# Channel-tile splits for the recurrence's input, long-convolution results kept in DRAM, and a new order of the seven Strassen products in a hybrid decoder layer

## The chip, the core and the metric

The kernel runs on one core of one Trainium2 chip. A core has five engines that take their instructions in parallel, each in its own order: TensorE (PE) for matrix products, VectorE (DVE), ScalarE (ACT), GpSimd (POOL), and SyncE (SP), which here only issues DMAs. The metric is the device time of one execution in microseconds (us), from a median of several runs. Work is in float32; each operand of a product is split into a high part (rounded to the type that TensorE takes) and a low remainder, and three products (high by high, high by low, low by high) stand for one.

## The reference, cut to what matters

One layer with 1024 positions and 1024 channels. The projection `z` has six parts, and two branches are computed from them:

```
h = rms_norm(x, g_mix)
z = h @ w_in + b_in
va, ga, xb, gb, sa, sb = split(z)          # 1024, 1024, 1536, 1536, 1024, 1024

u = causal_depthwise_conv(va * sigmoid(ga), conv_a_w)      # width 31
y_a = silu(layer_norm(u)) @ w_a_out

v = causal_depthwise_conv(xb, conv_b_w)                    # width 4
r, i = sigmoid(block_diag(v, w_a)), sigmoid(block_diag(v, w_x))   # 16 heads of 96 channels
v = linear_scan(a(r), mult(r) * i * v)                     # RG-LRU over the positions
y_b = (v * gelu(gb)) @ w_b_out

m = sigmoid(sa) * y_a + sigmoid(sb) * y_b
x = x + m @ w_o
x = x + square(relu(rms_norm(x) @ w_1)) @ w_2
out = rms_norm(x)
```

## The kernel before, in words

Channels lie on the 128 partitions and positions along a tile, so most tiles are 128x1024 (512 KB). They come from one pool, `acts`, with 35 buffers, which are given out in the order in which the program asks for them. A scheduler puts the instructions of each engine into one order ahead of time; `high_priority` and `high_priority(-LOWP)` move a block forward or back in it. At run time each engine and each issuing queue works through its order and waits where an input isn't there.

**First stage** (L367 to L561). `zchunk` (L377) makes 128 channels of `z` with 48 matmuls (8 slices of the contraction, three products, two halves) in one of three PSUM banks of tag `ps`. `xb_chunk` (L392) evacuates a chunk on ACT (L396) and applies the convolution of width 4: one pass on ACT (L399), three on VectorE (L404), result `v`, 12 tiles. `va_pair` (L493) makes a va and a ga chunk and joins them to `u` (L500 on ACT, L501 on VectorE). `conv` (L505) is the convolution of width 31: one pass on ACT (L513) and 30 passes, "taps", on VectorE (L516), each of which adds to the one before. The taps have low priority: they fill VectorE's gaps. Convolutions 0 to 4 start in this stage, 5 to 7 in the next. Each result, `y0` to `y7`, stays in a buffer of `acts` until the layer norm.

`rnn_steps` (L477) runs beside the chunks, a step after each. A head has 96 channels, which lie on one or two of the channel tiles (`PIECES`, L387). `rnn_load` (L415) moves the pieces of `v` into a 96x1024 tile of the pool `heads` (6 buffers) by DMAs on SP, and loads the head's weights. `rnn_split` (L427), one step later, splits the weights, and splits the head's input with `split_dma` (L64): ACT writes the negated high part, a DMA on POOL's queue adds the source to it, which leaves the low part, and ACT writes the high part again. `rnn_gates` (L436) has 12 matmuls (L444 to L446), two sigmoids (L448), and DMAs that bring the gates back to channel tiles (L453). `rnn_scan` (L455) does the recurrence for three channel tiles (four heads) at a time and stores the result in DRAM (`hd`).

**Strassen stage** (L566 to L694). The chunks of gb, sa and sb go in 14 pairs; each pair is one level of Strassen's scheme, in Winograd's form: seven products instead of eight, each 12 matmuls of 128x512 (`z_mm`, L624). The right-hand operands are the blocks of `h` and four sums of blocks, made by `x_sums` (L533) for each of two halves `c2`. The left-hand operands are made by `z_lhs` (L591): sums on VectorE (L598) and a split (L610 to L614). `z_step` (L652) issues a product, and after products 1 and 6 copies the bank on ACT into the bank on which later products accumulate (L656, L658). So product 6 needs the copy behind 1, and 5 and 3 the copy behind 6. `z_out` (L636) adds the bias, applies gelu or sigmoid, and stores to DRAM. The order of the products is written out by hand (`zseq`, L676 to L680); loads and left-hand operands are asked for up to four products ahead (L683). The pool `w` of this stage has 9 buffers, `evac` 5.

**yb and ya** (L696 to L798). `hg` is loaded from DRAM and split (12 tiles), and eight yb products run over it (L765 to L783). Between them stand three steps of the layer norm (`layer_norm_steps`, L727), behind yb 0, 3 and 5: the sum of the eight `y` on VectorE, the mean by a matmul with a constant matrix (`mu`) and the subtraction, the variance and the scaling. The last yb (L775) runs its three products slice by slice; the others use `mm3` (L85), which takes the low weights last. `split(ya[k], ...)` (L787) prepares the ya products (L788 to L795).

**Behind it** follow the output projection, the two products of the MLP (again Strassen's scheme) and the final norm.

Of the kernel before, what the change touches and what calls it, by code (L numbers as in the profile page):

```python
# [9 lines left out]
F32 = mybir.dt.float32  # L10
F32R = mybir.dt.float32r
# [19 lines left out]
def trunk_kernel(ctx: ExitStack, tc: tile.TileContext, x, xt_in, vecs, w_in, w_a_out, w_b_out,  # L31
# [13 lines left out]
    def T(name, dt=F32, shape=(P, S)):  # L45
        return tp.tile(list(shape), dt, tag="T", name=name)
# [4 lines left out]
    def split(src, h, l):  # L51
        nc.scalar.activation(h, src, AF.Copy)  # L52
        nc.vector.tensor_tensor(l, src, h.bitcast(F32), ALU.subtract)
# [10 lines left out]
    def split_dma(src, h, l):  # L64

        nc.scalar.activation(l, src, AF.Copy, scale=-1.0)  # L66
        nc.gpsimd.dma_start(l, src, accum_op=ALU.add)  # L67
        nc.scalar.activation(h, src, AF.Copy)
# [60 lines left out]
    def H(name, dt=F32):  # L129
        return qp.tile([HD, S], dt, tag="h", name=name)  # L130
# [278 lines left out]

    gws = {}  # L410
    parts = {}
    gate = {}
    hd = dp.tile([12, P, S], F32, name="hd")

    def rnn_load(n):  # L415
        g, hh = divmod(n, 4)
        v = H(f"v{n}")
        for (ti, p0, p1, d0) in PIECES[hh]:
            nc.sync.dma_start(v[d0:d0 + p1 - p0, :], vt[3 * g + ti][p0:p1, :])
        parts[n] = v  # L420
        raw = rp.tile([HD, 2, HD], F32, tag="rraw", name=f"rraw{n}")
        if n < 2:
            nc.gpsimd.tensor_copy(raw[0:1, 0, 0:1], vt[0][0:1, 0:1])
        nc.sync.dma_start(raw, w_rg[n])
        gws[n] = raw

    def rnn_split(n):  # L427
        gh = rp.tile([HD, 2, HD], F32R, tag="rh", name=f"rgh{n}")
        gl = rp.tile([HD, 2, HD], F32R, tag="rl", name=f"rgl{n}")
        split(gws[n], gh, gl)  # L430
        gws[n] = (gh, gl)
        vh, vl = H(f"vh{n}", F32R), H(f"vl{n}", F32R)
        split_dma(parts[n], vh, vl)
        parts[n] = vh, vl

    def rnn_gates(n):  # L436
        g, hh = divmod(n, 4)
# [39 lines left out]
    def rnn_steps():  # L477
        for n in range(-2, NH):
            if n >= 0:
                rnn_gates(n)  # L480
            if 0 <= n + 1 < NH:
                rnn_split(n + 1)
            if n + 2 < NH:
                while 3 * ((n + 2) // 4) + 2 not in vt:
                    yield
                rnn_load(n + 2)
            if n >= 0 and n % 4 == 3:
                rnn_scan(n // 4)
            yield

    ut, ya = {}, [None] * 8

    def va_pair(j):  # L493
        psv = zchunk(VA + j)
# [10 lines left out]
    def conv(j):  # L505
        u = ut.pop(j)
        acc = T(f"y{j}")

        def tap(d):
            w = WA - 1 - d  # L510
            return caw[:, w * 8 + j:w * 8 + j + 1]

        nc.scalar.activation(acc, u, AF.Identity, scale=tap(0), bias=cab_c[:, j:j + 1])  # L513
        with tc.high_priority(-LOWP):
            for d in range(1, WA):
                nc.vector.scalar_tensor_tensor(acc[:, d:S], u[:, 0:S - d], tap(d), acc[:, d:S],  # L516
                                               ALU.mult, ALU.add)
        ya[j] = acc

    rnn_it = rnn_steps()  # L520

# [8 lines left out]
    for p in (7, 6, 5, 4):  # L530
        xbh[p], xbl[p] = [None, None], [None, None]

    def x_sums(c2, last=()):  # L533
        q = {}
        for n, (hf, kk) in {12: (1, 0), 11: (0, 0), 22: (1, 1), 21: (0, 1)}.items():
            q[n] = wp.tile([P, S], F32, tag="w", name=f"xs{n}_{c2}") if n in last else \
                T(f"xs{n}_{c2}")
            nc.sync.dma_start(q[n], xu[hf, 2 * kk + c2])
        sub = nc.vector.tensor_tensor
        sub(q[11], q[12], q[11], ALU.subtract)  # L540
        sub(q[12], q[22], q[12], ALU.subtract)
        sub(q[22], q[22], q[11], ALU.subtract)
        sub(q[21], q[21], q[22], ALU.subtract)
        for p, n in ((7, 12), (6, 22), (5, 11), (4, 21)):
            xbh[p][c2] = h = T(f"xs{p}h_{c2}", F32R)
            nc.scalar.activation(h, q[n], AF.Copy)
            xbl[p][c2] = l = T(f"xs{p}l_{c2}", F32R)
            sub(l, q[n], h.bitcast(F32), ALU.subtract)

    for j in range(8):  # L550
        if j < 4:
            for i in range(3):
                xb_chunk(3 * j + i)
                step()
        va_pair(j)
        if j in CONVS:
            conv(CONVS[j])
        if j == 6:
            x_sums(0)
    for _ in rnn_it:  # L560
        pass  # L561

# [89 lines left out]
    def z_step(i, p):  # L652
        z_mm(i, p)
        with tc.high_priority():
# [17 lines left out]
                nc.vector.tensor_tensor(c, c, zb[i, "f"], ALU.add)  # L672
                z_out(i, 1, 0, c, "c")

    x_sums(1, (22, 21))
    zseq = [(0, 1), (1, 1), (0, 2), (1, 2), (0, 7), (0, 6), (0, 5), (1, 7), (0, 3), (0, 4),  # L676
            (1, 6), (1, 5)]
    for i in range(2, NZ):
        zseq += [(i, 1), (i - 1, 3), (i - 1, 4), (i, 7), (i, 6), (i, 2), (i, 5)]
    zseq += [(NZ - 1, 3), (NZ - 1, 4)]  # L680
    ready = 0
    for n, (i, p) in enumerate(zseq):
        while ready < min(len(zseq), n + 4):  # L683
            if zseq[ready][1] == 1:
                z_load(zseq[ready][0])
            z_lhs(*zseq[ready])
            ready += 1
        z_step(i, p)
        if p == 4 and i in (0, 2, 5):
            conv({0: 5, 2: 6, 5: 7}[i])  # L690
# [34 lines left out]
            hg.append((h, l))  # L725

    def layer_norm_steps():  # L727
        ssum = E("ssum")
        for j in range(1, 8):
            nc.vector.tensor_tensor(ssum, ya[0] if j == 1 else ssum, ya[j], ALU.add)  # L730
        yield
        pm = PS("mu", "ps2")
        for hs in HALVES:
            nc.tensor.matmul(pm[:, hs], onesm, ssum[:, hs], start=True, stop=True)
        vs, sq = E("vs"), E("sq")
        for j in range(8):
# [15 lines left out]
        yield  # L752

    ln_it = layer_norm_steps()
    wo = []

# [8 lines left out]
    for j in range(8):  # L765
        ws = wb0 if j == 0 else get_w(w_b_out[j, 0], f"wb{j}a") + get_w(w_b_out[j, 1], f"wb{j}b")
        sb = E(f"sb{j}")
        nc.gpsimd.dma_start(sb, spill[1, j])
        ps = PS(f"yb{j}")
        ops = [w + (wide(hg[k][0]), wide(hg[k][1])) for k, w in enumerate(ws)]  # L770
        if j < 7:
            mm3(ps, ops)
        else:

            for k, (wh, wl, ah, al) in enumerate(ops):  # L775
                for n, (a, b) in enumerate(((wh, ah), (wh, al), (wl, ah))):
                    for hf in range(2):
                        nc.tensor.matmul(ps[:, HALVES[hf]], a, b[hf], start=k == 0 and n == 0,
                                         stop=k == 11 and n == 2)
# [668 lines left out]
```

## Time and profile before

| what | value |
|---|---|
| median of 3 runs | 1702.7 us (1698.23 to 1703.65) |
| the profiled execution | 1702.45 us |
| its span, first to last instruction | 1700.6 us |
| mean granted clock of TensorE | 0.976 |
| ScalarE busy in the span | 891.1 us (52%) |
| GpSimd busy in the span | 214.5 us (13%) |
| first stage | to about 427 us |
| Strassen stage | about 427 to 735 us |
| yb, then ya | to about 885 and 985 us |

The span and the time of its own execution differ by 1.85 us, which lies before the first and after the last instruction. The page's rows for groups of instructions give the line, the engine, the operation, the written and the read names, the shapes, the count, the busy time and the mean duration in ns, and behind a bar the idle time of the engine just before them and what ended most of it. A row of the waits names who waited, for whom, the us in total, how often, and the longest. Where a helper records the instruction, the line is that of the helper: L92 is every `mm3`, L52 and L53 every `split`.

### The profile page before, as it was taken

How to read it: one execution, taken by the hardware profiler on the slowest of the kernel's cores; microseconds unless marked ns; L12 is line 12 of the kernel's file. 1: busy time of each engine (PE TensorE's matmuls, PEld its weight loads, DVE VectorE, ACT ScalarE, POOL GpSimd, SP SyncE). 2: the span in 40 equal slices, each digit the busy share in tenths (PEclk: the TensorE clock that was granted, in tenths of full speed). 3: DMA queues.
4: the chain of work that ended last, by engine and by line, in shares of the span. 5: the costliest groups of instructions: out<-in, count | busy, mean ns of one | idle time of the engine just before them, and what ended most of it. 6: DMA issues, size and time to landing. Idle time of an engine off the chain costs nothing. (4 is left out here: it accounts for less than half of the span.)

```text
span 1700.6 us, 18626 instructions
## 1 busy us (share of the span) xinstructions
PE 1601.7 (94%) x6910; PEld 1298.6 (76%) x6910; DVE 1146.5 (67%) x1329; ACT 891.1 (52%) x1157; POOL 214.5 (13%) x284
## 2 busy tenths in 40 slices
PE   8989889898799899989989999999999999999998
PEld 6867667677677677767868888778888888888886
DVE  6786788889988886354263315685555466888888
ACT  5548586773555555543354224564444457555553
POOL 0111010110223333311111000000000001111110
PEclk9989999999899999989999999999999999999999
DMA  9677776767587766773476255253332488888862
GB/s 364 147 159 176 170 177 141 188 142 224 130 217 204 184 162 168 175 248 100 101 214 175 74 149 173 79 182 124 112 112 99 138 261 205 216 231 213 217 142 99
DMA packets 94698, 288.63 MB, mean 170 GB/s; under 512 B 10976, under 2 KB 12512, under 8 KB 94608
## 3 DMA queue, kind: packets, MB, share of 16 engines
q1 hardware_dynamic: 59184, 180.77, 32.0%
q0 software_dynamic: 35280, 106.42, 29.6%
q8 instruction: 54, 0.88, 0.2%
q14 instruction: 36, 0.29, 0.1%
q10 hardware_dynamic: 144, 0.26, 0.0%
HBM read 139.82 MB, written 50.33 MB: 112 GB/s over the span
## 5 line engine op out<-in xcount | busy, mean ns | idle before, releaser
L516 DVE SCALAR_TENSOR_TENSOR y<-u,vec,y 128x1023 f32<-128x1023 f32 (+14 forms) x240 | 303.8, 1266 | 14.3 <-ACT y L513 10.2
L92 PE MATMUL z<-xh,win_h 128*128 128x512 f32 x400 | 131.0, 408 | 0.0
L92 PE MATMUL z<-xl,win_h 128*128 128x512 f32 x400 | 129.2, 403 | 0.0
L1244 DVE TENSOR_TENSOR acc<-acc,d 128x1024 f32<-128x1024 f32 x72 | 87.8, 1220 | 33.4 <-PE d L1232 32.8
L92 PE MATMUL z<-xh,win_l 128*128 128x512 f32 x400 | 94.8, 389 | 0.0
L92 PEld LDWEIGHTS z<-xh,win_h 128*128 128x128 f32 x400 | 79.6, 199 | 18.5 <-issue 0.2
L92 PEld LDWEIGHTS z<-xl,win_h 128*128 128x128 f32 x400 | 79.0, 197 | 18.1
L92 PEld LDWEIGHTS z<-xh,win_l 128*128 128x128 f32 x400 | 75.1, 188 | 15.6
L448 ACT ACTIVATE g<-rg,vec 96x1024 f32<-96x1024 f32 x32 | 35.6, 1112 | 65.1 <-PE rg L446 61.4
L446 PE MATMUL rg<-vl,rgh 96*96 96x512 f32 x64 | 29.2, 456 | 31.9 <-DMA vl<-v 31.9
L965 ACT ACTIVATE o<-s 128x512 fp32r<-128x512 f32 x64 | 38.1, 621 | 32.8 <-DVE s L957 28.2
L965 ACT ACTIVATE o<-w_raw 128x512 fp32r<-128x512 f32 x40 | 24.9, 624 | 51.7 <-DVE o L879 51.0
L781 DVE TENSOR_TENSOR m<-yb,sb 128x1024 f32<-128x1024 f32 x8 | 9.8, 1222 | 60.1 <-PE yb L92 47.7
L67 POOL DMA_DIRECT2D zo<-zw x42 | 37.1, 884 | 88.8 <-ACT zo L66 86.1
L67 POOL DMA_DIRECT2D db_1l<-wr x7 | 6.1, 867 | 327.2 <-ACT db_1l L66 304.7
L404 DVE SCALAR_TENSOR_TENSOR v<-xb,vec,v 128x1023 f32<-128x1023 f32 (+2 forms) x36 | 45.6, 1277 | 2.6 <-ACT v L399 2.6
L879 DVE TENSOR_TENSOR o<-s,o 128x512 fp32r<-128x512 f32 x64 | 42.4, 685 | 5.9 <-ACT o L965 5.8
L794 DVE TENSOR_TENSOR sa<-ya,sa 128x1024 f32<-128x1024 f32 x8 | 9.8, 1224 | 51.6 <-PE ya L92 51.6
L67 POOL DMA_DIRECT2D win_l<-win_raw x25 | 22.1, 883 | 176.8 <-ACT win_l L66 141.0
L863 DVE TENSOR_TENSOR x<-xr,o 128x1024 f32<-128x1024 f32 x8 | 9.7, 1219 | 51.4 <-PE o L831 37.2
L92 PE MATMUL ya<-suh,wa_h 128*128 128x512 f32 x128 | 40.0, 398 | 3.4 <-ACT suh L52 3.4
L446 PEld LDWEIGHTS rg<-vl,rgh 96*96 96x96 f32 x64 | 11.4, 178 | 41.5 <-DMA vl<-v 37.4
(1578 smaller groups left out, 4632.9 us busy)
## 6 DMA issues: line engine op xcount, KB each, us to landing
fr<-fd SPq DMA_DIRECT2D x32, 512.0 KB, 5.6
wr<-in_w_dram SPq DMA_DIRECT2D x32, 512.0 KB, 5.7
w_raw<-in_w_dram SPq DMA_DIRECT2D x31, 512.0 KB, 3.7
zw<-in_w_in_dram SPq DMA_DIRECT2D x28, 512.0 KB, 5.1
win_raw<-in_w_in_dram SPq DMA_DIRECT2D x25, 512.0 KB, 4.7
win_l<-win_raw POOLq DMA_DIRECT2D x25, 512.0 KB, 4.9
zo<-zw POOLq DMA_DIRECT2D x42, 256.0 KB, 3.6
fd<-fa SPq DMA_DIRECT2D x16, 512.0 KB, 3.3
```

The lines of the kernel that those rows point to most:

```text
L67: nc.gpsimd.dma_start(l, src, accum_op=ALU.add)
L92: nc.tensor.matmul(ps[:, HALVES[hf]], a, b[hf], start=i == 0, stop=i == len(todo) - 1)
L404: nc.vector.scalar_tensor_tensor(v[:, d:S], a[:, 0:S - d], cbw_c[:, w * 12 + t:w * 12 + t + 1], v[:, d:S], ALU.mult, ALU.add)
L446: nc.tensor.matmul(o, gh[:, gi, :], vl[:, hs], start=False, stop=True)
L448: nc.scalar.activation(a, ps[:HD, :], AF.Sigmoid, bias=(ba_c, bx_c)[gi][:, n:n + 1])
L516: nc.vector.scalar_tensor_tensor(acc[:, d:S], u[:, 0:S - d], tap(d), acc[:, d:S], ALU.mult, ALU.add)
L781: nc.vector.tensor_tensor(m[j], ps, sb, ALU.mult)
L794: nc.vector.tensor_tensor(sa, ps, sa, ALU.mult)
L863: nc.vector.tensor_tensor(x1, xr, ps, ALU.add)
L879: tt(l, src, h.bitcast(F32), ALU.subtract)
L965: nc.scalar.activation(o[:, 0], src, AF.Copy)
L1244: tt(acc[p, q2], acc[p, q2], ps, ALU.add)
```

## The change

It has four parts.

1. `rnn_load` splits each of the 12 tiles of `v` on the channel tiles (ACT copy, VectorE subtraction) and moves both parts to the heads' tiles by DMAs on SP. `rnn_split` is gone; the split of the heads' weights is in `rnn_load`, a step earlier.
2. `conv` stores each `y` in DRAM (`yd`) and adds it to `ysum` (for conv 0, an ACT copy starts it). The layer norm takes `ysum` for the mean and loads the `y` again as `yn`. It has two steps, behind yb 1 and 4.
3. `x_sums(0)` comes one pair earlier, `x_sums(1)` at the end of the first stage. In the Strassen stage the order of the seven products changes, loads are asked for seven products ahead, and the pools have 8 and 7 buffers for 9 and 5.
4. The last yb uses `mm3` too; three of the split tiles of ya take buffers of the pool `late`; one PSUM tag behind ya changes.

```diff
     def rnn_load(n):
         g, hh = divmod(n, 4)
-        v = H(f"v{n}")
+        parts[n] = H(f"vh{n}", F32R), H(f"vl{n}", F32R)
         for (ti, p0, p1, d0) in PIECES[hh]:
-            nc.sync.dma_start(v[d0:d0 + p1 - p0, :], vt[3 * g + ti][p0:p1, :])
-        parts[n] = v
+            t = 3 * g + ti
+            if t not in vp_:
+                vp_[t] = T(f"vth{t}", F32R), T(f"vtl{t}", F32R)
+                split(vt[t], *vp_[t])
+            for a, b in zip(parts[n], vp_[t]):
+                nc.sync.dma_start(a[d0:d0 + p1 - p0, :].bitcast(F32), b[p0:p1, :].bitcast(F32))
         raw = rp.tile([HD, 2, HD], F32, tag="rraw", name=f"rraw{n}")
...
-        gws[n] = raw
-
-    def rnn_split(n):
         gh = rp.tile([HD, 2, HD], F32R, tag="rh", name=f"rgh{n}")
         gl = rp.tile([HD, 2, HD], F32R, tag="rl", name=f"rgl{n}")
-        split(gws[n], gh, gl)
+        split(raw, gh, gl)
         gws[n] = (gh, gl)
-        vh, vl = H(f"vh{n}", F32R), H(f"vl{n}", F32R)
-        split_dma(parts[n], vh, vl)
-        parts[n] = vh, vl
...
         for n in range(-2, NH):
             if n >= 0:
                 rnn_gates(n)
-            if 0 <= n + 1 < NH:
-                rnn_split(n + 1)
             if n + 2 < NH:
...
             for d in range(1, WA):
                 nc.vector.scalar_tensor_tensor(acc[:, d:S], u[:, 0:S - d], tap(d), acc[:, d:S],
                                                ALU.mult, ALU.add)
-        ya[j] = acc
+            nc.sync.dma_start(yd[j], acc)
+            if j == 0:
+                ysum.append(T("ysum"))
+                nc.scalar.activation(ysum[0], acc, AF.Copy)
+            else:
+                nc.vector.tensor_tensor(ysum[0], ysum[0], acc, ALU.add)
...
-        for p, n in ((7, 12), (6, 22), (5, 11), (4, 21)):
+        for p, n in ((6, 22), (7, 12), (5, 11), (4, 21)):
...
-        if j == 6:
+        if j == 5:
             x_sums(0)
     for _ in rnn_it:
         pass
+    x_sums(1)
...
-    wp = stage.enter_context(tc.tile_pool(name="weights2", bufs=9, reuse_waits="tile"))
+    wp = stage.enter_context(tc.tile_pool(name="weights2", bufs=8, reuse_waits="tile"))
...
-    vp = stage.enter_context(tc.tile_pool(name="evac", bufs=5, reuse_waits="tile"))
+    vp = stage.enter_context(tc.tile_pool(name="evac", bufs=7, reuse_waits="tile"))
...
-    x_sums(1, (22, 21))
-    zseq = [(0, 1), (1, 1), (0, 2), (1, 2), (0, 7), (0, 6), (0, 5), (1, 7), (0, 3), (0, 4),
-            (1, 6), (1, 5)]
+    zseq = [(0, 1), (1, 1), (0, 2), (1, 2), (0, 6), (0, 7), (1, 7), (0, 5), (1, 6), (0, 3), (0, 4),
+            (1, 5)]
     for i in range(2, NZ):
-        zseq += [(i, 1), (i - 1, 3), (i - 1, 4), (i, 7), (i, 6), (i, 2), (i, 5)]
+        zseq += [(i, 1), (i, 7), (i - 1, 3), (i, 6), (i, 2), (i - 1, 4), (i, 5)]
     zseq += [(NZ - 1, 3), (NZ - 1, 4)]
-    ready = 0
+    loaded = ready = 0
     for n, (i, p) in enumerate(zseq):
+        while loaded < min(len(zseq), n + 7):
+            if zseq[loaded][1] == 1:
+                z_load(zseq[loaded][0])
+            loaded += 1
         while ready < min(len(zseq), n + 4):
-            if zseq[ready][1] == 1:
-                z_load(zseq[ready][0])
             z_lhs(*zseq[ready])
...
     def layer_norm_steps():
-        ssum = E("ssum")
-        for j in range(1, 8):
-            nc.vector.tensor_tensor(ssum, ya[0] if j == 1 else ssum, ya[j], ALU.add)
-        yield
         pm = PS("mu", "ps2")
         for hs in HALVES:
-            nc.tensor.matmul(pm[:, hs], onesm, ssum[:, hs], start=True, stop=True)
+            nc.tensor.matmul(pm[:, hs], onesm, ysum[0][:, hs], start=True, stop=True)
         vs, sq = E("vs"), E("sq")
         for j in range(8):
+            ya.append(T(f"yn{j}"))
+            nc.sync.dma_start(ya[j], yd[j])
...
-        ops = [w + (wide(hg[k][0]), wide(hg[k][1])) for k, w in enumerate(ws)]
-        if j < 7:
-            mm3(ps, ops)
-        else:
-
-            for k, (wh, wl, ah, al) in enumerate(ops):
-                for n, (a, b) in enumerate(((wh, ah), (wh, al), (wl, ah))):
...
+        mm3(ps, [w + (wide(hg[k][0]), wide(hg[k][1])) for k, w in enumerate(ws)])
...
-        if j in (0, 3, 5):
-            next(ln_it)
+        if j in (1, 4):
+            next(ln_it, None)
     su = []
     for k in range(8):
-        su.append((T(f"suh{k}", F32R), T(f"sul{k}", F32R)))
+        su.append(((E if k < 2 else T)(f"suh{k}", F32R), (E if k < 1 else T)(f"sul{k}", F32R)))
...
-            ps = PS(f"tr_m0{kk}{c2}", "ps2" if kk else "ps")
+            ps = PS(f"tr_m0{kk}{c2}", "ps2" if kk and c2 else "ps")
```

More of the change, by code (lines that the diff above doesn't have):

```diff
@@ L411, in trunk_kernel @@
     parts = {}
+    vp_ = {}
     gate = {}
@@ L489, in rnn_steps @@
             yield
-    ut, ya = {}, [None] * 8
+    ut = {}
+    yd = dp.tile([8, P, S], F32, name="yd")
+    ysum = []
     def va_pair(j):
@@ L531, in trunk_kernel, with x_sums @@
         xbh[p], xbl[p] = [None, None], [None, None]
-    def x_sums(c2, last=()):
+    def x_sums(c2):
         q = {}
         for n, (hf, kk) in {12: (1, 0), 11: (0, 0), 22: (1, 1), 21: (0, 1)}.items():
-            q[n] = wp.tile([P, S], F32, tag="w", name=f"xs{n}_{c2}") if n in last else \
-                T(f"xs{n}_{c2}")
+            q[n] = T(f"xs{n}_{c2}")
             nc.sync.dma_start(q[n], xu[hf, 2 * kk + c2])
@@ L751, in layer_norm_steps @@
                                  bias=lnb_c[:, j:j + 1])
-        yield
+    ya = []
     ln_it = layer_norm_steps()
@@ L769, in trunk_kernel @@
         ps = PS(f"yb{j}")
-        ops = [w + (wide(hg[k][0]), wide(hg[k][1])) for k, w in enumerate(ws)]
-        if j < 7:
-            mm3(ps, ops)
-        else:
-            for k, (wh, wl, ah, al) in enumerate(ops):
-                for n, (a, b) in enumerate(((wh, ah), (wh, al), (wl, ah))):
-                    for hf in range(2):
-                        nc.tensor.matmul(ps[:, HALVES[hf]], a, b[hf], start=k == 0 and n == 0,
-                                         stop=k == 11 and n == 2)
+        mm3(ps, [w + (wide(hg[k][0]), wide(hg[k][1])) for k, w in enumerate(ws)])
         m.append(T(f"m{j}"))
         nc.vector.tensor_tensor(m[j], ps, sb, ALU.mult)
-        if j in (0, 3, 5):
-            next(ln_it)
+        if j in (1, 4):
+            next(ln_it, None)
     su = []
     for k in range(8):
-        su.append((T(f"suh{k}", F32R), T(f"sul{k}", F32R)))
+        su.append(((E if k < 2 else T)(f"suh{k}", F32R), (E if k < 1 else T)(f"sul{k}", F32R)))
         split(ya[k], *su[k])
```

## The prediction

> **What bounds the kernel now.** I read the page first: the busy shares, the 40 slices and the costliest groups.
>
> ```profile
> span 1700.6 us, 18626 instructions
> PE 1601.7 (94%) x6910; PEld 1298.6 (76%) x6910; DVE 1146.5 (67%) x1329; ACT 891.1 (52%) x1157; POOL 214.5 (13%) x284
> ...
> PE   8989889898799899989989999999999999999998
> ...
> DVE  6786788889988886354263315685555466888888
> ...
> L516 DVE SCALAR_TENSOR_TENSOR y<-u,vec,y 128x1023 f32<-128x1023 f32 (+14 forms) x240 | 303.8, 1266 | 14.3 <-ACT y L513 10.2
> ...
> L446 PE MATMUL rg<-vl,rgh 96*96 96x512 f32 x64 | 29.2, 456 | 31.9 <-DMA vl<-v 31.9
> ```
>
> TensorE sets the end: its slices are full from the 23rd on. What the change can reach lies before that. There VectorE stands at 8 and 9 tenths over ten slices (about 210 to 640 us), so the 67% of the page hides a stage in which VectorE is nearly as full as TensorE. The second view is that of the waits of TensorE.
>
> ```profile
> PE rg L446 <- DMA vl<-v: 31.9, 12, 5.2
> PE z1a L632 <- ACT zo L68: 7.3, 1, 7.3
> ...
> PE z0a L632 <- DVE u L501: 7.0, 1, 7.0
> PE yb L92 <- ACT hgh L52: 4.4, 2, 3.2
> PE ya L92 <- ACT suh L52: 3.4, 1, 3.4
> PE z1e L632 <- ACT z1e L658: 3.1, 1, 3.1
> ...
> PE yb L92 <- ACT wb1a_h L68: 2.1, 1, 2.1
> PE yb L778 <- DMA wb7a_l<-wb7a_raw: 1.7, 1, 1.7
> ...
> PE yb L778 <- DMA wb7b_l<-wb7b_raw: 1.2, 1, 1.2
> ```
>
> The third cuts the time at events that both kernels have: u0, v8, u7, then the sums of pairs 4, 9 and 13 of the Strassen products, and the end of the ya products. Columns: stretch, PE, PEld, DVE, ACT, POOL busy, granted clock, DMA share, GB/s.
>
> ```profile
> 75.57:206.34 130.77, 116.90 (x474) 90.87 (x473) 96.40 (x86) 78.95 (x81) 13.59 (x16) 0.93 0.73 167
> 206.34:427.26 220.92, 195.47 (x814) 154.22 (x812) 191.98 (x167) 146.31 (x141) 18.86 (x22) 0.95 0.68 175
> 427.26:541.20 113.94, 100.83 (x413) 81.09 (x414) 100.54 (x115) 63.71 (x109) 33.00 (x44) 0.92 0.68 172
> 541.20:651.30 110.10, 101.82 (x432) 81.04 (x431) 94.08 (x102) 59.86 (x105) 34.58 (x47) 0.99 0.67 175
> 651.30:728.20 76.90, 72.72 (x313) 58.09 (x312) 30.39 (x39) 43.03 (x75) 23.12 (x32) 1.00 0.73 197
> ```
>
> ```profile
> 728.20:985.00 256.80, 242.90 (x1028) 196.52 (x1029) 109.58 (x97) 99.56 (x112) 33.98 (x46) 0.97 0.55 150
> ```
>
> TensorE's loss in a stretch is its idle time plus (1 - clock) times the stretch. In order: 13.9 + 9.2 = 23.1, 25.5 + 11.0 = 36.5, 13.1 + 9.1 = 22.2, 8.3 + 1.1 = 9.4, 4.2, and 13.9 + 7.7 = 21.6 us: 117 us in all, the most that could be won. In the second stretch TensorE alone would need 220.9 - 36.5 = 184 us, VectorE 192. **VectorE is the bound there as soon as TensorE's waits go.**
>
> **The heads' input.** Removed: 16 accumulating DMAs on POOL's queue and 32 copies of 96x1024 on ACT. Added: 12 copies on ACT, 12 subtractions on VectorE, and twice the moves on SP (48 for 24). The bytes stay, since the accumulation read what the second move now carries.
>
> ```profile
> vl<-v POOLq DMA_DIRECT2D x15, 384.0 KB, 6.7
> ...
> v<-v SPq DMA_DIRECT2D x7, 384.0 KB, 5.3
> ```
>
> Today the accumulation for head n+1 is issued behind the gates of head n, and lands 6.7 us later; that is the 31.9 us. In the changed kernel both parts of head n+2 move into buffers that head n has left, a whole step earlier, and 5.3 us fit into it. So I let that wait go. It shrinks what TensorE loses; what ends the stage is next.
>
> **The long convolution's block.** The changed kernel takes the sum's buffer from the pool of activations behind the first convolution. The instruction order shows it: ACT's copy of y0 to the sum stands ahead of the evacuation of z19 (xb3), z20 and z21, and VectorE issues conv 0's 30 taps in one run with one small subtraction inside. On SP the store of y0 stands ahead of the gates' moves of head 0. Rows for it: VectorE's taps today, the evacuation of z20, and 16 matmuls of a chunk.
>
> ```profile
> 76.89 9.18 DVE L516 SCALAR_TENSOR_TENSOR y<-u,vec,y 128x1023 f32<-128x1023 f32 x7 [1.31 <-ACT y L513]
> ...
> 113.00 0.36 DVE L53 TENSOR_TENSOR rgl<-rraw,rgh 96x192 fp32r<-96x192 f32 x1 [5.89 <-ACT rgh L52]
> 113.27 3.86 DVE L516 SCALAR_TENSOR_TENSOR y<-u,vec,y 128x1006 f32<-128x1006 f32 x3
> ```
>
> ```profile
> 97.75 1.11 ACT L396 ACTIVATE xb<-z,vec 128x1024 f32<-128x1024 f32 x1 [2.56 <-PE z L92]
> 98.77 1.05 ACT L66 ACTIVATE win_l<-win_raw 128x1024 fp32r<-128x1024 f32 x1
> ```
>
> ```profile
> 93.93 3.79 PE L92 MATMUL z<-xh,win_l 128*128 128x512 f32 x16
> ```
>
> Seven taps in 9.18 us are 1.31 each. Thirty end at 76.9 + 39.4 + 0.3 = 116.6; the copy of y0 (1.05, the size of the row at 98.77) and xb3 (1.11) end at 118.8. TensorE has three banks for chunks: z20 is done at 97.7, z21 one chunk later (48 matmuls, 3 x 3.79 less the overlap = 10.9, and one gate's six at that rate, 1.4), at 110. z1 then waits for xb3: about 9 us. The row at 113.00 shows that an engine's order holds: VectorE idled 5.89 us for rgh although the taps behind it had their input.
> The Trainium skill, "TensorE: Matmul & The Clock Gate", Part 1 (Architectural detail), says that the queues of ScalarE and VectorE are strictly first in, first out; the row agrees. By that rule the 9 us come; were ACT to pass xb3 ahead, the time would be some 6 us lower than below.
>
> Against it stand the six waits for vl that fall into this stretch (13.4 us of the 31.9), and their half clock:
>
> ```profile
> 96.00:116.00 20.00, 16.91 (x63) 12.98 (x62) 13.94 (x13) 8.62 (x9) 1.70 (x2) 0.83 0.75 144
> ```
>
> The six are in a later row of the same view, cut to this stretch:
>
> ```profile
> PE rg L446 <- DMA vl<-v: 13.4, 6, 3.5
> ```
>
> A clock of 0.83 over 20 us is 6.8 us at half rate behind one wait: 3.4 us lost. The stretch's loss of 23 becomes the 9 us of z1, some 4 of clock behind it, and some 7 where heads' gates and chunk 23 wait for an ACT that is late by then: 20. I take a gain of **3 us** at v8 (206.3 becomes 203), between -10 (no block) and +8 (the block and the late head moves both count in full).
> The Trainium skill, same page, Part 1 ("HAM oscillation"), says that a gap over about 3.4 us drops the clock to half for a window of that length. The trace agrees (0.83 above). It speaks against a single wait of 9 us: by it two windows at half rate follow, 3.4 us, which is inside my 4.
>
> **From v8 to u7.** VectorE's in-order work today is the 192.0 us of the second row. From the order of the changed kernel's instructions between the same two: 85 taps for 87, 4 subtractions more, 3 additions to the sum more. A pass over 128x1024 costs
>
> ```profile
> L460 DVE TENSOR_TENSOR g<-g,v 128x1024 f32<-128x1024 f32 x12 | 14.7, 1222 | 15.0 <-DMA g<-g 14.8
> ```
>
> So +7 x 1.22 - 2 x 1.27 = +6.0, or 198.0 us. TensorE's 184 are less, so VectorE ends last. Its idle time today is 220.9 - 192.0 = 28.9, and part of it is
>
> ```profile
> DVE rgl L53 <- ACT rgh L52: 9.5, 3, 6.4
> DVE u L501 <- ACT u L500: 5.6, 3, 2.6
> DVE y L516 <- ACT y L513: 5.4, 2, 2.7
> ```
>
> The first goes mostly (the split of the heads' weights moves a step earlier), the second too, as TensorE is ahead. I keep 14 of 28.9, half; bounds 5 and 29. u7 ends at 203 + 198 + 14 = 415, for 427.3: **-12**, of which 3 from above. z0a's wait grows from 7.0 to about 10: TensorE gets there first.
>
> **The seven products.** In the new order two products (about 5.4 us) lie between each copy on ACT and the product that adds to it, where today it is one or none. That removes small waits such as z1e's 3.1 in the third and fourth stretch. But VectorE has 100.5 + 94.1 = 194.6 us of work in these 224.0, and the changed order puts 4 taps and 4 additions to the sum there: +10, 204.6. Its idle time of 29.4 is partly
>
> ```profile
> DVE zs L598 <- DMA zw<-in_w_in_dram: 35.7, 10, 8.9
> DVE zc L666 <- ACT zc L665: 17.1, 6, 4.2
> ```
>
> (half of both lies behind 651 us). The loads are asked for three products earlier, but the ring has one buffer less, and each load still waits for a product of the pair before. I keep 15: 219.6, a gain of **4.5**; bounds 210 (5 of idle) and 234 (all of it stays). z1a's 7.3 stays: it needs x_sums(1) behind u7. From pair 10 on TensorE is the bound (72.7 of 76.9): nothing.
>
> **yb and ya.** DRAM takes y instead of the pool: 8 stores and 8 loads of 512 KB, 4 us each beside products of 16 us. The buffers let wb0 and the first hg come before the last pair. The 7 additions of ssum leave VectorE, which is idle there for over half of the time: nothing. The last yb no longer needs its low parts at once (-1.7 - 1.2), LN is a step earlier (-3.4 at ya), wb1a_h -2.1: 8.4; hgh and the clock's 7.7 I leave but for 0.6. **-9**, bounds 0 and -21. Behind it TensorE is full: nothing.
>
> **Sum.** Span 1700.6 - 12.3 - 4.5 - 9 = 1674.8, and 1.85 us outside it (the profiled execution took 1702.45): 1676.6. That run lies 0.25 below the median of 1702.7, so it needs no shift. Forecast **1676**.
>
> **Rivals.**
> *VectorE's gaps stay* (slower). Its work grows by 6.0 to u7 and 10 to pair 9. If its idle 28.9 and 29.4 are waits for ACT and DMA that the change leaves (rgh, y, zw, zc), u7 ends at 203 + 198 + 28.9 = 430 (+2.6) and pair 9 takes 234 (+10); with -5 at yb that is 1710. It decides from the point where VectorE's idle time between v8 and pair 9 stays over some 47 of its 58 us. For it: the zs and zc rows; against: rgl and u above, which wait for TensorE's own delay.
> *VectorE runs nearly without a gap* (faster): u7 at 203 + 198 + 6 = 407 (-20), the pairs to 9 in 210 (-14), yb and ya -15: 1653. For it: taps of low priority stand behind all that waits. Against: the block early, and zw.
> *The heads still wait*: the change doesn't do what it says, because SP issues in order and its moves stand behind the gates' moves, which wait most of all there:
>
> ```profile
> SPq L453 <- ACT g L448: 120.4, 24, 10.7
> ```
>
> Then TensorE keeps some 20 of 31.9 and VectorE's gaps with it; u7 at about 427, z -1, yb -7: 1695.
>
> **Numbers.** Forecast 0.45 (its own range 1664 to 1690), gapless 0.17, heads wait 0.13, gaps stay 0.25. A measurement tells 0.3%, 5.1 us, from no change. Faster: 0.45 + 0.17 + two thirds of 0.13 = 0.70; slower: most of the last, 0.22; the rest 0.08. The range goes from 1650 to 1712: it takes in all the cases' centres and leaves out both tails.
>
> **What would show it.** Right: no rows of rg waiting for vl over some 3 us in all; a wait of 7 to 11 us of z1 for xb (ACT L396) near 110, with a low clock behind it; VectorE over 90% busy from v8 to u7; z0a waiting for u about 10 us; u7 near 415; no waits of z..e for ACT; wb7a_l gone from the list. Wrong: u7 later than 425, waits of rg on moves by SP, VectorE below 85% between u7 and pair 9, yn loads that hold wb4 up, or gains behind 985.

## The result, and the profile after

The changed kernel takes 1662.47 us (median; 1661.07 to 1662.79) against 1702.97 us of the kernel before on the same chip. The ratio is 0.9766, with a 95% interval of 0.9748 to 0.9785: 40 us less. The forecast was 1676 and its range 1650 to 1712. So the direction and the range held, and the gain of 26.7 us came out 14 us too small. The profiled execution took 1662.79 us, its span is 1661.0, TensorE's mean clock 0.983.

The page of the changed kernel, the rows that answer to those shown of before:

```profile
span 1661.0 us, 18664 instructions
PE 1588.0 (96%) x6910; PEld 1291.0 (78%) x6910; DVE 1155.5 (70%) x1341; ACT 870.9 (52%) x1135; POOL 201.4 (12%) x268
...
PE   8979899997899999989999999999999999999997
...
DVE  6784999999989995325533224875555367888888
...
L516 DVE SCALAR_TENSOR_TENSOR y<-u,vec,y 128x1009 f32<-128x1009 f32 (+22 forms) x240 | 299.8, 1264 | 6.1 <-ACT y L513 2.6
```

VectorE's slices now show 9 from the fifth to the fifteenth but for one 8 (about 166 to 623 us), where they showed a 7 and a mix of 8 and 9. The 4 in front of them, the fourth slice (125 to 166 us), was a 6. The waits of TensorE in the changed kernel:

```profile
PE z L92 <- ACT xb L396: 9.2, 1, 9.2
PE rg L444 <- ACT g L448: 7.1, 4, 5.1
...
PE z L92 <- ACT u L500: 6.6, 2, 5.8
PE z1a L637 <- ACT zo L68: 6.2, 1, 6.2
PE z0a L637 <- DVE u L501: 3.8, 1, 3.8
PE yb L92 <- ACT hgh L52: 3.6, 2, 2.4
...
PE rg L446 <- DMA vl<-vtl: 1.7, 1, 1.7
```

The wait for vl fell from 31.9 to 1.7 us. At the top stands a wait that wasn't there before: a chunk waits 9.2 us for xb. The timelines of ACT and of TensorE show where:

```profile
118.01 1.06 ACT L521 ACTIVATE ysum<-y 128x1024 f32<-128x1024 f32 x1 [6.04 <-DVE y L516]
118.97 1.10 ACT L396 ACTIVATE xb<-z,vec 128x1024 f32<-128x1024 f32 x1
```

```profile
120.12 1.22 PE L92 MATMUL z<-xh,win_h 128*128 128x512 f32 x2 [9.25 <-ACT xb L396]
```

ACT's copy of y0 waits for the thirtieth tap, the evacuation of z19 stands behind the copy, and TensorE, whose three banks are full, stands behind that. The cuts at the same events (end of u0, v8, end of u7, the sums of pairs 4, 9, 13, end of ya), columns as before:

```profile
76.38:210.82 134.44, 118.85 (x494) 93.14 (x493) 102.61 (x90) 73.50 (x74) 7.74 (x9) 0.92 0.66 166
210.82:407.95 197.13, 184.51 (x794) 146.61 (x792) 195.44 (x172) 127.64 (x124) 12.20 (x14) 0.98 0.73 202
407.95:520.55 112.60, 99.88 (x410) 78.98 (x411) 104.02 (x118) 64.39 (x107) 31.69 (x42) 0.94 0.68 178
520.55:624.15 103.60, 97.96 (x427) 79.13 (x426) 94.36 (x105) 60.90 (x104) 33.41 (x45) 1.00 0.79 208
624.15:703.35 79.20, 76.10 (x325) 61.59 (x324) 36.75 (x45) 49.28 (x83) 25.76 (x35) 0.98 0.78 210
703.35:947.00 243.65, 238.92 (x1027) 193.79 (x1026) 97.15 (x87) 97.20 (x109) 34.94 (x47) 0.99 0.61 170
```

Against the rows of before: the first stretch is 3.7 us longer, the second 23.8 shorter, the third 1.3, the fourth 6.5 shorter, the fifth 2.3 longer, the last 13.2 shorter. In the second VectorE is busy 195.4 of 197.1 us.

### The profile page after: what moved, and what is told of

Same layout as the page of the kernel before. It is cut to its first block, busy times and chain, and to the rows that moved or that the text cites. A ratio compares the mean times of both kernels' runs of the same rounds, so it can differ in the third digit from the quotient of the medians.

```text
span 1661.0 us, 18664 instructions
## 1 busy us (share of the span) xinstructions
PE 1588.0 (96%) x6910; PEld 1291.0 (78%) x6910; DVE 1155.5 (70%) x1341; ACT 870.9 (52%) x1135; POOL 201.4 (12%) x268
## 4 chain that ended last, share of the span: by engine, by line
PE 73%; DVE 14%; DMA 6%; issue 4%; ACT 3%; POOL 0%; SPq 0%; DVEq 0%; POOLq 0%; ACTq 0%
PE d L1228 14%; PE yb L92 7%; DVE y L516 7%; PE z L92 6%; PE ya L92 5%; PE o L827 3%; PE e L1343 2%; PE keep L1228 2%; PE o L92 2%; DMA zo<-zw 2%; PE z L257 2%; DMA zo<-zs 1%; DVE g L474 1%; DMA hg<-hgd 1%; DVE v L404 1%
## 5 line engine op out<-in xcount | busy, mean ns | idle before, releaser
L516 DVE SCALAR_TENSOR_TENSOR y<-u,vec,y 128x1009 f32<-128x1009 f32 (+22 forms) x240 | 299.8, 1264 | 6.1 <-ACT y L513 2.6
L92 PE MATMUL z<-xh,win_h 128*128 128x512 f32 x400 | 127.2, 399 | 15.8 <-ACT xb L396 9.2
L1240 DVE TENSOR_TENSOR acc<-acc,d 128x1024 f32<-128x1024 f32 x72 | 87.8, 1219 | 33.4 <-PE d L1228 32.7
L92 PEld LDWEIGHTS z<-xl,win_h 128*128 128x128 f32 x400 | 76.8, 192 | 17.1
L68 ACT ACTIVATE win_h<-win_raw 128x1024 fp32r<-128x1024 f32 x25 | 26.3, 1056 | 43.7 <-PE z L92 37.3
L875 DVE TENSOR_TENSOR o<-s,o 128x512 fp32r<-128x512 f32 x64 | 42.4, 684 | 5.9 <-ACT o L961 5.8
L118 ACT ACTIVATE xn<-x 128x1024 f32<-128x1024 f32 x8 | 8.5, 1057 | 58.8 <-DVE x L859 58.8
```

The costliest lines, as they stand in the source:

```text
L92: nc.tensor.matmul(ps[:, HALVES[hf]], a, b[hf], start=i == 0, stop=i == len(todo) - 1)
L875: tt(l, src, h.bitcast(F32), ALU.subtract)
L1240: tt(acc[p, q2], acc[p, q2], ps, ALU.add)
```

## The experiments

Two theories were set against each other. **A:** from u0 to the sum of pair 9 the time is VectorE's work plus VectorE's gaps, and what the change saves there is gaps. **B:** TensorE's waits set the time, each counts by itself, and VectorE has room. One row of each kernel decides: the stretch from the end of u0 to pair 9, with VectorE's busy time in it. The rows come with the runs; a table at the end puts them together. For the two kernels themselves they are, before and then changed:

```profile
75.57:651.27 575.70, 514.98 (x2130) 407.22 (x2128) 482.96 (x464) 348.83 (x434) 100.01 (x128) 0.95 0.69 173
```

```profile
76.38:624.11 547.73, 501.16 (x2121) 397.81 (x2120) 496.39 (x480) 326.42 (x408) 85.03 (x110) 0.96 0.71 189
```

VectorE's work grew from 483.0 to 496.4 us, its gaps fell from 92.7 to 51.3.

Each row is of one execution. The kernel before took 1691 to 1709 us beside these runs, so a few us in a row prove nothing alone, and a difference between two kernels by their ratios is uncertain by 5 to 8 us. The forecasts start from 1702.7 us for the kernel before and 1662 us for the changed one where they name no other time; what is compared with them is the difference.

### The parts alone: e_heads, e_dram, e_order

The kernel before with `rnn_load` of the change and without `rnn_split` (part 1):

```diff
-            if 0 <= n + 1 < NH:
-                rnn_split(n + 1)
```

> The kernel before with the first part of the change alone: the splits of v on channel tiles, both parts moved to heads a step early. Theory A (up to the ninth Strassen pair VectorE's work and the gaps in it set the time): the waits of rg for vl go (31.9 us), VectorE gets 12 subtractions (14.7 us), so u7 comes where VectorE's work ends with few gaps, about 14 us earlier (412), and most of that stays to the end: 1683 to 1692. Theory B (each wait taken from TensorE's list comes back in full, with its half clock): about 1658 to 1670. Theory C (the gain of the whole change is the Strassen stage's and yb's): 1700 or more.

```profile
75.55:617.83 542.28, 499.82 (x2125) 398.56 (x2124) 492.54 (x472) 326.13 (x410) 87.54 (x113) 0.97 0.69 182
```

1673.0 us, ratio 0.9851 (0.9817 to 0.9886), 25 us less than before on that chip: between the figures of A and B. Gaps fell by 43, work rose by 9.6, and pair 9 came 33.4 us earlier; behind it 5.8 us were given back.

The kernel before with part 2 and the yb stage:

```diff
-        ya[j] = acc
+            nc.sync.dma_start(yd[j], acc)
+            if j == 0:
+                ysum.append(T("ysum"))
+                nc.scalar.activation(ysum[0], acc, AF.Copy)
...
-        if j in (0, 3, 5):
-            next(ln_it)
+        if j in (1, 4):
+            next(ln_it, None)
```

> The kernel before with the second part alone: y to DRAM, the sum beside the convolutions, the layer norm's two steps behind yb 1 and 4, the last yb like the others. Theory A: the block of conv 0's 30 taps comes here too (z1 waits about 9 us near 110), while VectorE's gaps behind it take it up in part; VectorE gets 7 additions earlier; the Strassen stage is the same; yb and ya gain 8 to 13. Together 1692 to 1702. Theory B: -13 at yb and ya, +9 for z1's wait with 3 of clock: 1701 and no change before yb.

TensorE's waits, and the stretch:

```profile
PE rg L446 <- DMA vl<-v: 27.5, 11, 4.7
PE z L92 <- ACT xb L396: 8.2, 1, 8.2
```

```profile
76.52:656.25 579.73, 513.31 (x2125) 404.54 (x2124) 489.25 (x471) 351.23 (x437) 100.26 (x128) 0.95 0.70 181
```

1699.4 us, ratio 1.0009 (0.9989 to 1.0029): no difference, as B had it and as A had it at its upper end. The block comes here as well (8.2 us), pair 9 is 5.0 us later, and from pair 9 to the end the time is 13.7 us shorter: a loss and a gain of one part that nearly cancel. The profiled execution took 1693.7 us, the shortest of ten: it lies 8.7 us below the profiled one of before, the medians differ by 1.0. In a median run the loss is larger or the gain smaller than these rows show.

The kernel before with part 3:

```diff
-        zseq += [(i, 1), (i - 1, 3), (i - 1, 4), (i, 7), (i, 6), (i, 2), (i, 5)]
+        zseq += [(i, 1), (i, 7), (i - 1, 3), (i, 6), (i, 2), (i - 1, 4), (i, 5)]
...
-        if j == 6:
+        if j == 5:
             x_sums(0)
```

> The kernel before with the third part alone: earlier sums of x, the new order of the seven products, loads seven ahead. Theory A: u7 stays at 426 within 3 us, from there to pair 9 some 5 to 8 us less, the rest as before: 1694 to 1698. Theory B: all small waits of z..e for ACT go, 17 us, and their clock: 1683 to 1688.

```profile
75.38:629.38 554.00, 505.77 (x2118) 401.66 (x2117) 485.81 (x468) 349.03 (x430) 97.70 (x125) 0.96 0.70 178
```

1680.1 us, ratio 0.9896 (0.9863 to 0.9928), 18 us less: what B had (15 to 20), twice what A had at most. From z0a to the sum of pair 13 it took 281.4 us for 300.8 before. In the changed kernel that stretch took 295.2, so most of this gain did not show there. That became a question of its own (a_own_x below). Part 3 is more than the new order: the sums of x, the loads and the pools change too, and none of them was run alone.

### Without the block: a_own

```diff
             if j == 0:
-                ysum.append(T("ysum"))
-                nc.scalar.activation(ysum[0], acc, AF.Copy)
+                ysum.append(acc)
```

> The changed kernel, but the sum of the y lies in y0's own buffer from the start: no copy of y0 on ACT and no buffer of its own. Same result. The block goes: z1 no longer waits 9 us near 110, and conv 0's taps lie between other work as before. Theory A: VectorE had 32 us of gaps before v8, and TensorE's stall made part of them; with TensorE 9 to 13 us earlier at z24 VectorE starts earlier on what follows, but has conv 0's taps still to do; u7 5 us earlier, end 1656 to 1659. Theory B: the whole wait and its clock come back: 1649 to 1652.

```profile
75.70:616.38 540.68, 501.70 (x2123) 400.26 (x2122) 498.27 (x480) 327.13 (x408) 84.92 (x110) 0.97 0.72 192
```

1646.8 us, ratio 0.9698 (0.9656 to 0.974), which is 11.5 us below the changed kernel by the ratios. My size was wrong and B's was right for the whole. That the wait of 9 us and its half clock come back in full is not shown: pair 9 comes 7.7 us earlier, and some 6 us more come between pairs 10 and 13, whose cause is not settled. VectorE's gaps fall by 8.9 to pair 9, so the block had left VectorE without input too. The edit takes away the copy and the buffer at once; which of the two made the block was not separated.

### Work added: a_max and e_max

```diff
             nc.vector.scalar_tensor_tensor(v[:, d:S], a[:, 0:S - d], ...
+        nc.vector.tensor_tensor(v, v, v, ALU.max)
```

> The changed kernel with one idle pass more on VectorE for each of the 12 tiles of v (the tile's maximum with itself, 128x1024, about 1.22 us each, 14.7 us in all, 5 of it behind v8). The output is the same. Theory A (from u0 to u7 VectorE has almost no gaps of its own, so its work sets u7): the passes behind z1's wait near 110 fall in full on u7, 9 to 14 us later, and 7 to 14 of it stay to the end: 1669 to 1677. Theory B (TensorE's waits set the time, VectorE has room): u7 0 to 4 us later, end 1662 to 1666.

```profile
75.66:630.76 555.10, 506.37 (x2120) 401.63 (x2119) 506.08 (x488) 328.35 (x409) 85.03 (x110) 0.96 0.71 187
```

1667.3 us, ratio 0.9807 (0.978 to 0.9835), 7 us above the changed kernel by the ratios: at A's lower edge, with an uncertainty of 6 that takes in B's 4 as well. Three of the twelve passes lie ahead of the end of u0 and one tap moved behind pair 9, so the work in the stretch rose by 9.7; the gaps fell by 2.3.

> The kernel before with the same 12 idle passes (14.7 us of VectorE). The output is the same. Theory A: VectorE has 28.9 us of gaps between v8 and u7 here and 34 before v8, and the passes go into them in part: 2 to 7 us more, 1700 to 1707 where before stands at 1699. Theory B: nothing, within 2 us. If the passes cost all of their 14.7 us here too, the gaps are not free and my split into work and gaps falls.

```profile
76.09:656.08 579.99, 514.85 (x2130) 406.77 (x2128) 490.57 (x472) 349.70 (x434) 100.11 (x128) 0.95 0.68 171
```

1713.1 us, ratio 1.0072 (1.0043 to 1.01), 12 to 13 us of 14.7. Here I was wrong, and by the condition that I had set: the gaps of before are hardly room. Work in the stretch rose by 7.6, gaps fell by 3.3 alone. Pair 9 came 4.8 us later; the rest of the 13 us arose behind it, and why is not shown.

### Work taken away: a_taps

```diff
-            for d in range(1, WA):
+            for d in range(1, WA - 8 if j in (3, 4) else WA):
```

> The changed kernel with 8 taps left out of each of the long convolutions 3 and 4 (16 passes on VectorE, 20.3 us, all behind v8; these two results are not the reference's). Theory A (from u0 to pair 9 the time is VectorE's work plus its gaps; 500 + 49 us in the changed kernel): the scheduler lets other taps move up, so u7 gains only some 5 us, but pair 9 comes 12 to 20 us earlier, and most of it stays: 1645 to 1652 where the changed kernel has 1662. Theory B (TensorE's waits for ACT, DMA and the banks set the time, VectorE follows): 0 to 4 us, 1658 to 1662.

```profile
75.62:617.94 542.32, 499.89 (x2123) 398.75 (x2122) 491.04 (x476) 325.76 (x408) 85.22 (x110) 0.97 0.72 192
```

1653.6 us, ratio 0.9753 (0.9717 to 0.9789). Pair 9 came 6 us earlier, and neither theory had that. The row says why: taps of later convolutions moved up into most of the 16 places, so the work in the stretch fell by 5.4 us only, and with gaps of 51.3, the same to a tenth, the stretch fell by 5.4 too. That is A's sum, with a size that I had read from the number of taps and not from the order. The whole time is only 2 us below the changed kernel by the ratios, 4 by the medians, inside the noise: the figure that B had.

### Subtractions off VectorE: a_own_acc

```diff
-                split(vt[t], *vp_[t])
+                split_dma(vt[t], *vp_[t])
```

> The changed kernel with the sum in y0's own buffer, and with the low part of each tile of v made as the weights' is: ACT writes the negated high part, POOL's queue adds the source, ACT writes the high part. VectorE loses 12 subtractions (14.7 us), ACT gets 12 copies, POOL's queue 12 accumulations of 512 KB (4.9 us each) ahead of the moves. Same result. Theory A: u7 6 to 12 us earlier than without it, end 1638 to 1642 where the one with the sum in y0's buffer has 1647. Theory B: 1645 to 1648. Theory C (the moves come later by the accumulation and the wait for vl is back): 1650 or more, with rows of rg waiting for vl.

The stretch, and then a wait of TensorE, of VectorE and of SP's queue, each from the view of its own:

```profile
75.17:622.61 547.44, 502.23 (x2118) 400.92 (x2117) 490.28 (x473) 337.88 (x420) 93.74 (x120) 0.96 0.78 201
```

```profile
PE rg L444 <- ACT g L448: 14.5, 4, 8.8
```

```profile
DVE g L460 <- DMA g<-g: 16.3, 4, 11.7
```

```profile
SPq L426 <- DMA vtl<-v: 22.6, 5, 7.3
```

1660.4 us, ratio 0.9765 (0.9741 to 0.979), 11 us worse by the ratios than a_own: theory C in size, by another path. VectorE lost 8.0 us of work to pair 9 and got 14.8 us of gaps. The moves of the heads wait 22.6 us on SP for the accumulations, the moves of the gates stand behind them, and VectorE waits for the gates up to 11.7 us at once. That chain explains this longest wait, at 145 us, only in part: ahead of the last of its moves (issued at 137.3) SP had waited 3.7 us for an accumulation of v, and 5.0 us for one of the weights, which POOL had issued behind two of v. rg did not wait for vl.

### Where the sums of x stand: a_own_x, a_x, a_own_x2

With a_own's edit, and besides:

```diff
-        if j == 5:
-            x_sums(0)
+        if j in (5, 6):
+            x_sums(j - 5)
     for _ in rnn_it:
         pass
-    x_sums(1)
```

> The changed kernel with the sum in y0's own buffer, and with the second sums of x asked for behind pair 6, so that their 8 VectorE passes stand ahead of u7. Same result. Theory A: u7 and z0a 4 to 8 us later, z1a's wait of 7.1 gone, VectorE's work the same: within 3 us of 1647. Theory B (each wait of TensorE counts for itself): z1a's 7.1 comes back with its half clock while z0a's wait grows by as much: the same too. Rival D: u7 keeps its time, since VectorE's taps stand behind the sums: 1639 to 1642.

```profile
75.38:597.68 522.30, 493.49 (x2115) 395.62 (x2114) 491.35 (x478) 326.60 (x408) 84.94 (x110) 0.98 0.75 197
```

```profile
PE z0a L635 <- ACT zo L68: 8.2, 1, 8.2
```

1637.05 us, ratio 0.9623 (0.9598 to 0.9648): the best of all, 24 us below the changed kernel by the ratios. A and B had both said "the same"; the rival gave 1639 to 1642, and the gain on a_own is 13 us by the ratios where the rival had 5 to 8. u7 moved by 2.0 us, z1a's wait went (z0a's grew to 8.2), the work fell by 6.9 (taps moved behind pair 9, where VectorE is idle for half of the time) and the gaps by 11.4.

From z0a to pair 13 it took 281.7 us, what e_order took. It would be tempting to say that the order needs sums that are ready at its start. e_order itself speaks against that. There, and then in the changed kernel, the first product of the stage and the first pass of the second sums:

```profile
422.87 0.77 PE L632 MATMUL z0a<-xh,zo 128*128 128x512 f32 x1 [4.66 <-DVE u L501]
```

```profile
427.73 1.22 DVE L539 TENSOR_TENSOR xs<-xs,xs 128x1024 f32<-128x1024 f32 x1
```

```profile
408.09 0.47 PE L637 MATMUL z0a<-xh,zo 128*128 128x512 f32 x1 [3.76 <-DVE u L501]
```

```profile
411.65 1.22 DVE L544 TENSOR_TENSOR xs<-xs,xs 128x1024 f32<-128x1024 f32 x1
```

In e_order the sums begin 4.9 us behind z0a, in the changed kernel 3.6, yet e_order takes 281.4 us and the changed kernel 295.2. What the changed kernel loses there, and why earlier sums win it back, stays open.

The same on the changed kernel, with the block:

> The changed kernel with the second sums of x asked for behind pair 6, and the sum of the y as the change has it (with the block of conv 0). Same result. If the block and the start of the Strassen stage are two separate losses of VectorE's time, this gains the 10 to 12 us that it gained on top of the other: 1650 to 1653. If the block's delay was cover for the start (VectorE behind its work), 1655 to 1660.

```profile
75.05:612.41 537.36, 496.65 (x2115) 395.99 (x2114) 490.56 (x475) 326.20 (x408) 84.75 (x110) 0.97 0.72 192
```

1651.1 us, ratio 0.9726 (0.9698 to 0.9753). By the time alone that is the first branch, 1650 to 1653. But this chip ran the kernel before 4.5 us faster than the changed kernel's chip did, and by the ratios the gain is 7 us, the second branch. Without the block the same edit gained 13. With an uncertainty of 6 and 8 us the two agree: that the two losses are wholly separate is possible and not shown.

A pair earlier still (`if j in (4, 5): x_sums(j - 4)`):

> The changed kernel with the sum of the y in y0's buffer and the sums of x asked for behind pairs 4 and 5 (a pair earlier than in the best one so far). Same result. VectorE's work is the same, and the sums stand farther ahead of u7 than before, so ACT no longer stands before the first Strassen operand waiting for a sum (8.2 us of z0a's wait). Theory A: the gap of VectorE there is small already, so 0 to 4 us less than the 1637 of the best so far. Theory B: 5 to 8 us less, 1629 to 1632. Rival: the pool of 35 buffers is full a pair earlier, and chunks wait for buffers: 1640 or more.

```profile
76.22:617.97 541.75, 500.12 (x2118) 398.81 (x2117) 506.88 (x488) 326.27 (x407) 85.08 (x110) 0.97 0.72 191
```

```profile
PE z L92 <- ACT u L500: 20.4, 5, 11.8
```

ACT at the end of that longest wait of 11.8 us:

```profile
361.42 1.28 ACT L500 ACT_TABLE_LOAD   x1
362.71 1.11 ACT L500 ACTIVATE u<-z,vec 128x1024 f32<-128x1024 f32 x1
```

1653.5 us, ratio 0.9753 (0.9725 to 0.9781): 22 us worse than a_own_x by the ratios, as the rival had it, and in the main not for its reason. VectorE had more work ahead of pair 9 (506.9 for 491.4), most of it ahead of u7 (12.2), and chunks waited up to 11.8 us for the joining of an earlier pair. In that wait ACT did not stand: from 352.1 to 362.7 us it ran a weight's split, the recurrence's activations (L464 to L468) and four table loads of 1.28 us each, which stand ahead of the joining in this kernel's order. The next wait of a chunk, 4.4 us at 392, is in part the rival's: there ACT waits twice (1.6 and 1.1 us) for passes that read the sums before it writes another tile (L549, L500), which is a wait for a buffer as far as the names tell.

### All together

From the end of u0 to pair 9, in us; the last column is the median less that of the kernel before on the same chip.

| kernel | VectorE's work | gaps | stretch | whole time |
|---|---|---|---|---|
| before | 483.0 | 92.7 | 575.7 | |
| e_dram | 489.3 | 90.5 | 579.7 | +1.0 |
| e_max | 490.6 | 89.4 | 580.0 | +13.2 |
| e_order | 485.8 | 68.2 | 554.0 | -18.3 |
| e_heads | 492.5 | 49.7 | 542.3 | -25.4 |
| changed | 496.4 | 51.3 | 547.7 | -40.5 |
| a_taps | 491.0 | 51.3 | 542.3 | -44.9 |
| a_max | 506.1 | 49.0 | 555.1 | -32.5 |
| a_own | 498.3 | 42.4 | 540.7 | -51.6 |
| a_own_acc | 490.3 | 57.2 | 547.4 | -39.5 |
| a_x | 490.6 | 46.8 | 537.4 | -47.4 |
| a_own_x2 | 506.9 | 34.9 | 541.8 | -45.0 |
| a_own_x | 491.4 | 31.0 | 522.3 | -62.8 |

The three parts alone give -25.4, +1.0 and -18.3 us, in sum -42.7 for the -40.5 of the change: within the noise they add up.

That work and gaps add up to the stretch is true by definition. What the runs show is that the two move by different edits. Three edits of work alone (a_taps, a_max, e_max: -5.4, +9.7, +7.6) changed the gaps by 0.0, -2.3 and -3.3. The edits of waits and order changed the gaps by up to 62 and the work by less than 24. So neither theory stands as it was put. A's sum is right, but its gaps are little room: they took up 2.3 of 9.7 and 3.3 of 7.6 us. That B's waits of TensorE are the other side of the same gaps, so that the time is lost for both engines, is how I read it; no run separates it.

## Why the prediction was right, and where its sizes were off

**VectorE as the bound.** Right: over 90% busy from v8 to u7 was forecast, 99% was measured.

**The heads' wait.** Right: 31.9 to 1.7 us. The 7.1 us in which gates wait for ACT to empty the bank of the gates before (rg for g) were forecast too: 6.3 of them lie ahead of v8, where "some 7" stood for gates and a chunk that wait for a late ACT.

**The block of conv 0.** Right in place and price: forecast 9 us with xb3 done at 118.8, measured 9.25 with xb3 done at 120.1 (u0 came 0.8 later). The timelines show the copy that waits for the last tap; that the sum's buffer is what brings the taps forward was read from the order, and no run separates it from the copy. The half clock behind the wait was put at some 4 us; the row from 120 to 140 us shows a clock of 0.85, that is 3.0 us lost:

```profile
120.00:140.00 20.00, 19.88 (x75) 15.27 (x76) 14.31 (x13) 13.88 (x16) 0.87 (x1) 0.85 0.63 172
```

The Trainium skill, "TensorE: Matmul & The Clock Gate", Part 1, "HAM oscillation", says that an idle gap of more than about 3.4 us brings the clock down to half. The trace agrees again: 9.25 us of wait, and 0.85 behind it. The two windows that the forecast let follow are its own count, not that section's.

The stretch to v8 was mis-sized all the same. A gain of 3 us was forecast; the evacuation of z24 stood at 203.0, as before, and v8's first pass at 210.8 for 206.3, since VectorE was behind. TensorE's loss there is 15.6 us of idle time and 10.8 of clock, 26 for the 20 forecast.

**From v8 to u7: the step that was mis-sized.** "I keep 14 of 28.9, half" of VectorE's gaps. The gaps were 1.7 (197.1 less 195.4), below the lower bound of 5. The work was 195.4 for 198.0. u7 ended at 408.0 for 415 as forecast, and that is in part luck: v8 was 7.8 us late against the forecast and the stretch behind it 14.9 short. In a_own, without the block, the same stretch has 5.5 of gaps, so some 4 of the missing 12 went with the block; that a VectorE that is behind finds its input ready is how I read it. The others went with part 1: e_heads alone has 4.6, where e_dram has 25.5 and e_order 27.2.

```profile
189.51:391.73 202.22, 188.21 (x814) 150.42 (x812) 197.60 (x172) 132.40 (x128) 12.21 (x15) 0.99 0.70 192
```

The forecast had kept half of the gaps as waits that the change leaves; most of them hung on the heads' input. z0a's wait went to 3.8 and not up to 10: TensorE was not ahead.

**The seven products.** Forecast 219.6 us from u7 to pair 9 (204.6 of work, 15 of gaps); measured 216.2 (198.4 and 17.8). Here the work was over-counted by 6. (Of the 17.1 us of the zc row, 15.3 lie behind 651 us, not half.) For pairs 10 to 13 nothing was forecast and they took 2.3 us more. e_order shows what the forecast did not look for: part 3 alone takes 19 us from z0a to pair 13. The change as made got 6 of them against the kernel before, and 11 against part 1 alone, which takes 306.6 there.

**yb and ya.** Forecast -9, measured -13.1 from pair 13 to the last ya (248.9 to 235.8), and 1.6 more to the end where nothing was forecast. The waits went as named (suh, wb7a, wb7b gone, wb1a at 0.3, hgh at 3.6). The clock's 7.7 us, of which only 0.6 were counted, is where the rest lies: 0.99 over 243.7 us loses 2.4. The runs show that this belongs to the change and not to the one execution. The four kernels with the old yb stage (before, e_max, e_order, e_heads) took 249 to 251 us there at a clock of 0.96 to 0.98, the nine with the new one 233 to 236 at 0.99 to 1.00; the kernel before and e_dram:

```profile
728.20:977.10 248.90, 235.00 (x993) 189.99 (x994) 105.33 (x92) 94.35 (x105) 32.40 (x45) 0.97 0.54 147
```

```profile
735.70:968.70 233.00, 229.12 (x992) 186.66 (x991) 93.35 (x83) 91.92 (x102) 33.28 (x45) 0.99 0.60 168
```

The loads of yn held nothing up.

**The rivals.** "Nearly without a gap" had u7 at 407, and 408 is what came; behind it the Strassen stage to pair 9 gave half of what it said (-7.8 for -14), yb and ya nearly all (-13.1 for -15), and pairs 10 to 13 took 2.3 back, so that its 1653 was 9 us too low, as the forecast of 1676 was 14 too high. "Gaps stay" and "the heads still wait" fell.

## What to carry to other kernels

A copy of the result of low-priority work, put on an engine that has urgent work behind it, holds that work up: here one copy, with one buffer taken from the shared pool, cost some 11 us, and the instruction order showed it ahead of any run. Where two engines are nearly equally full, count the fuller one's work and its gaps apart, and look for the edit that starts its input earlier; a gap took up little added work here, and work moved off the engine is worth nothing if it returns as a wait (a_own_acc). Compare runs of different chips by the difference from the same kernel on each: two verdicts here turn on it (e_order, a_x).

## What the runs showed of the hardware that had not been expected

How much longer moves take beside accumulations. In a_own, from 74 to 395 us, and then in a_own_acc, with 12 accumulations of 512 KB more:

```profile
win_l<-win_raw POOLq DMA_DIRECT2D x22, 512.0 KB, 4.6
...
g<-g SPq DMA_DIRECT2D x16, 384.0 KB, 4.4
...
g<-g SPq DMA_DIRECT2D x16, 256.0 KB, 5.3
...
vh<-vth SPq DMA_DIRECT2D x7, 384.0 KB, 4.3
```

```profile
g<-g SPq DMA_DIRECT2D x16, 384.0 KB, 6.4
...
vtl<-v POOLq DMA_DIRECT2D x10, 512.0 KB, 7.9
g<-g SPq DMA_DIRECT2D x16, 256.0 KB, 5.3
...
vh<-vth SPq DMA_DIRECT2D x7, 384.0 KB, 6.5
```

The mean DMA share over these 321 us rises from 0.73 to 0.83, and the median of these moves of 384 KB by half, from 4.3 and 4.4 to 6.5 and 6.4 us; an accumulation takes 7.9. It does not hold for every transfer: the moves of 256 KB of the gates stay at 5.3, and in the changed kernel, without the accumulations, the same two moves of 384 KB take 5.6 and 5.0 us at a share of 0.72. How much of the rise is the share's is not shown.
